# The first two modulation vectors of a two-block transformer: summed without a stop, with products of zeros between their sums over partitions

## The chip, the cores and the metric

The kernel runs on one core of a Trainium2 chip. The metric is device time of one execution in microseconds (us); lower is better. The engines go by the profile's names: PE is the tensor engine (PEld its loads of stationary operands), DVE the vector engine, ACT the scalar engine, POOL the GpSimd engine, and SPq, POOLq and ACTq are the queues from which transfers are issued. Each engine works through its own list of instructions in the order of the program and waits where an operand is not there yet.

## What is computed

Two transformer blocks of two layers each work on 256 tokens of width 1024. Each layer has a mixer and a feed-forward part, and ahead of each of them the normalized activations are scaled and shifted by vectors that come from a condition `c`:

```python
def modulation(c, w, b):
    m = jnp.einsum("bd,de->be", jax.nn.silu(c), w) + b
    shift, scale, gate = jnp.split(m, 3, axis=-1)
...
x = layer_norm(x, ln0_g, ln0_b)
for layer in range(DEPTH):
    shift, scale, gate = modulation(c, ada_w[layer, 0], ada_b[layer, 0])
    h = x * (1.0 + scale) + shift
    y = hybrid_mixer(h, ...)
    x = layer_norm(DN_ALPHA * x + (1.0 + gate) * y, ...)
    ...
```

The first mixer cannot begin before the first `scale` and `shift` are known. Each is a product of a vector of 1024 with a matrix of 1024 x 1024, that is 4 MB of `ada_w` in float32.

## The kernel before

Nine steps follow each other: step 0 is the start (constants, `x`, its layer norm, the first two vectors), steps 1 to 8 are the mixers and feed-forward parts. Nothing of step 1's products can run before step 0's vectors are there.

A vector is made in two parts. `mod_rows` (L282) loads a tile of two 128-row slices of `ada_w` (1 MB, one of four buffers `raw`), and DVE multiplies each slice by its 128 values of silu(`c`) (`csil`) and adds it to the accumulator `macc`: the first slice with a TENSOR_SCALAR (L300), the other seven with a SCALAR_TENSOR_TENSOR (L302), each over 128 x 1024 elements. Then `mod_done` (L304) sums `macc` over the partitions with eight products with a column of ones on PE (L329 to L331, shown under the helper's line L179), and DVE adds the bias to the eight columns (L335, tile `col`). In step 0 `scale` goes first, then `shift`. A `raw` buffer is free again when DVE has read it, so the transfer of a later tile, `w_in` of the mixer among them, waits for DVE.

`setup` (L343) loads the constants and the many small vectors. POOL issues the transfers of most of them, row by row into stacked tiles `sh`; PE transposes each stack (L183) and DVE copies it into a tile of columns (L387): `col3` at once, and `col1`, `col2`, `col4` after the generator's `yield`. `col1` holds the layer norm's gains, which the mixer's scale needs. Behind them stand a mask (`maskb`: a MEMSET on POOL, L410, then two CASTs of DVE into it, L411 and L412) and a few small operations.

In step 1 `ab` (L517) makes A and B from the two vectors and `col1` (L524, L528, L529), `make_h` (L494) makes the mixer's input `h` from the transposed activations (ACT L511 and L513, DVE L509 and L514), and `proj_nat` begins with the products L174 to L176 of `h` with the first tile of `w_in`, which ACT and DVE have split into `hi` (L155) and `lo` (L156).

The program's text does not fix the order on each engine: a scheduler takes instructions by the place of their text, by priorities set around it and by its own costs, and that order is then fixed for the chip. A transfer that POOL issues goes on one of eight semaphores in turn, so the ninth waits until the first has landed.

Of the kernel before, what the change touches and what calls it, by code (L numbers as in the profile page):

```python
# [14 lines left out]
ACT = mybir.ActivationFunctionType  # L15
ALU = mybir.AluOpType
# [4 lines left out]
KD = 8  # L21
# [42 lines left out]
class _Net:  # L64
# [111 lines left out]
        mm(out, lhsT=a[1], rhs=b[0], start=False, stop=stop)  # L176

    def mm(self, out, lhsT, rhs, start=True, stop=True):
        self.nc.tensor.matmul(out, lhsT=lhsT, rhs=rhs, start=start, stop=stop)  # L179

    def tr(self, out, in_):
        p = in_.shape[0]
# [96 lines left out]
        if k0 == 4:  # L279
            self.plus(key, g[:, hs], self.modps)  # L280

    def mod_rows(self, key):  # L282

        nc = self.nc
        V = nc.vector
        w, b, j, c0 = self.mod_src(key)
        row = key[2] == "gate"
        if self.modpos == 0:
            self.modacc = self.tl("macc", [128, D])
            if row:  # L290
                nc.gpsimd.memset(self.modacc, 0.0)
                nc.gpsimd.dma_start(out=self.modacc[0:1, :], in_=b[j * D:(j + 1) * D].unsqueeze(0))
        acc = self.modacc
        wv = w.rearrange("(k p) n -> p k n", p=128)
        v = self.raw(wv[:, self.modpos:self.modpos + 2, j * D:(j + 1) * D])
        for i in range(2):
            k = self.modpos + i
            c = self.csil[:, c0 + k:c0 + k + 1]
            if k == 0 and not row:
                V.tensor_scalar(acc, v[:, i], c, None, ALU.mult)  # L300
            else:
                V.scalar_tensor_tensor(acc, v[:, i], c, acc, ALU.mult, ALU.add)  # L302

    def mod_done(self, key):  # L304

        if key in self.gates_pe:
            return self.modacc
        l, s, name = key
        j, acc = self.mod_src(key)[2], self.modacc
        if name == "gate":  # L310
            g = self.tl("gate", [128, D])
            for h in range(2):
                hs = slice(h * 512, (h + 1) * 512)
                p = self.ps(pool=self.mps)
                self.mm(p, self.ones, acc[:, hs])
                self.plus(key, g[:, hs], p)
            return g
        c = self.tl("col", [128, KD])
        if self.step in (2, 6):

            sums = self.sc([128, KD])
            for k in range(0, KD, 4):
                p = self.ps((128, 4, 128), pool=self.mps)
                for q in range(4):
                    self.tr(p[:, q], acc[:, (k + q) * 128:(k + q + 1) * 128])
                for q in range(4):
                    self.nc.scalar.activation(p[:, q], p[:, q], ACT.Copy, accum_out=sums[:, k + q:k + q + 1])
        else:
            p = self.ps(pool=self.mps)  # L329
            for k in range(KD):  # L330
                self.mm(p[:, k:k + 1], acc[:, k * 128:(k + 1) * 128], self.ones[:, 0:1])  # L331
            sums = p[:, 0:KD]
        q = ((l * 2 + s) * 3 + j) * KD if l < 2 else ((l - 2) * 6 + j) * KD
        bc = (self.col3 if l < 2 else self.col4)[:, q:q + KD]
        self.nc.vector.scalar_tensor_tensor(c, sums, 1.0 if name == "scale" else 0.0, bc, ALU.add, ALU.add)  # L335
        return c

    def mod(self, l, s, name):
        assert (l, s, name) in self.mods, (l, s, name)
        return self.mods[(l, s, name)]  # L340


    def setup(self):  # L343
        nc, a = self.nc, self.a
        S, V = nc.scalar, nc.vector
        cr = self.tl("const", [16, 128], tag="cr")
        S.dma_start(out=cr[0:8], in_=a["c"].rearrange("b (k p) -> (b k) p", p=128))
        S.dma_start(out=cr[8:16], in_=a["c_2"].rearrange("b (k p) -> (b k) p", p=128))
        cst = self.tl("const", [128, C_END], tag="cst")
        nc.sync.dma_start(out=cst, in_=a["consts"])  # L350
        self.ident = cst[:, C_ID:C_LE]
        self.tri_le = cst[:, C_LE:C_LT]
        self.tri_lt = cst[:, C_LT:C_NEG]
        self.rt = cst[:, C_RT:C_COS]
        self.cosn = cst[:, C_COS:C_SIN].rearrange("p (t d) -> p t d", t=2)
        self.sinn = cst[:, C_SIN:C_INV].rearrange("p (t d) -> p t d", t=2)
        self.cst_inv = cst[:, C_INV:C_IOTA]
        self.iota = cst[:, C_IOTA:C_TIE]
        self.tie = cst[:, C_TIE:C_END]
        self.ones = self.tl("const", [128, 128], tag="ones")  # L360
        nc.gpsimd.memset(self.ones, 1.0)
        self.zero = self.tl("const", [128, 128], BF16, tag="zero")
        nc.gpsimd.memset(self.zero, 0.0)
        p = self.ps()
        self.tr(p[:, 0:16], cr)
        self.csil = self.tl("const", [128, 16], tag="csil")
        S.activation(self.csil, p[:, 0:16], ACT.Silu)
        self.off = {}

        def stack(tag, names, eng):  # L370

            r = self.sc([128, 128])
            q = 0
            for name in names:
                ap = a[name]
                n = int(np.prod(ap.shape)) // 128
                lead = " ".join("abc"[:len(ap.shape) - 1])
                eng.dma_start(out=r[q:q + n], in_=ap.rearrange(f"{lead} (k p) -> ({lead} k) p", p=128))
                self.off[name] = q
                q += n  # L380
            return r, q

        def columns(tag, r, q):
            p = self.ps()
            self.tr(p[:, 0:q], r[:q])
            c = self.tl("const", [128, q], tag=tag)
            V.tensor_copy(c, p[:, 0:q])  # L387
            return c

        self.col3 = columns("col3", *stack("col3", ("ada_b",), S))  # L390
        r1 = stack("col1", ("ln0_g", "ln0_b", "post_ln_g", "post_ln_b", "norm_mix_2", "norm_ffn_2"), nc.gpsimd)
        r2, q = stack("col2", ("ssd_conv_w", "ssd_conv_b", "ssd_norm_w", "mla_q_norm", "mla_kv_norm", "gm_b_s"), nc.gpsimd)
        q0 = q
        for name in ("moba_q_norm_2", "moba_k_norm_2", "diff_q_norm_2", "diff_k_norm_2", "moba_out_norm_2"):
            for r in range(2):
                nc.gpsimd.dma_start(out=r2[q:q + 2, r * 64:(r + 1) * 64], in_=a[name])
            self.off[name] = q
            q += 2
        nc.gpsimd.dma_start(out=r2[q:q + 2], in_=a["diff_subln_2"])
        self.off["diff_subln_2"] = q  # L400
        q += 2
        r4 = stack("col4", ("b_mod_2",), nc.gpsimd)
        yield
        self.col1 = columns("col1", *r1)
        self.col2 = columns("col2", r2, q)
        self.col4 = columns("col4", *r4)
        self.identb = self.tl("const", [128, 128], BF16, tag="identb")
        V.tensor_copy(self.identb, self.ident)
        self.maskb = self.tl("const", [128, 384], BF16, tag="maskb")
        nc.gpsimd.memset(self.maskb, 0.0)  # L410
        V.tensor_copy(self.maskb[:, 0:128], cst[:, C_NEG:C_RT])  # L411
        V.tensor_copy(self.maskb[:, 256:384], cst[:, C_NEG:C_RT])  # L412
        o = self.off
        V.tensor_scalar(self.col2[:, 0:60], self.col2[:, 0:60], 0.5, None, ALU.mult)
        q0, q1 = o["moba_q_norm_2"], o["moba_out_norm_2"]
        for b in (0, 64):
            V.memset(self.col2[b:b + 16, q0:q1], 1.0)
        for l in range(2):
            c = o["diff_subln_2"] + l
            V.tensor_scalar(self.col2[:, c:c + 1], self.col2[:, c:c + 1], 1.0 - self.lam_init(l), None, ALU.mult)  # L420
# [1075 lines left out]
    def run(self):  # L1496
        a, nc = self.a, self.nc
# [7 lines left out]

        SC, SH, GA = "scale", "shift", "gate"
        plan = {
            0: [(0, 0, SC), (0, 0, SH)],
            1: [(0, 0, GA), (0, 1, SC), (0, 1, SH)],
            2: [(0, 1, GA), (1, 0, SC), (1, 0, SH), (1, 0, GA), (1, 1, SC), (1, 1, SH)],  # L1510
            3: [(1, 1, GA)],
# [9 lines left out]
        with self.phase(sh=12, s1=1, s2=3, pp=4, pa=4):  # L1521
            setup = self.setup()
            next(setup)
            self.mod_start(plan[0])
            x = self.load_x(a["x"])
            xn = x = self.layer_norm(x)
            self.fill(KD * KD)
            for _ in setup:
                pass
            g, b = self.c1("ln0_g", 0), self.c1("ln0_b", 0)  # L1530
            self.later = [lambda x=x: self.affine(x, a["ln0_g"], a["ln0_b"])]
        for s in range(1, 9):
# [5 lines left out]
            with self.phase(**SIZES[s]):  # L1538
# [18 lines left out]
                    get = lambda t, hh: ysum[t][hh]  # L1557
                else:
                    h = self.make_h(xn, A, B)
                    self.mod_start(plan.get(s, []), LAG.get(s, 0))  # L1560
                    if i == 0:
                        get = self.mixer(l, h, FILL[s]) if one else self.attn2(l - 2, h)
# [48 lines left out]
```

## Time and profile before

| | us |
|---|---|
| median of 3 runs | 2075.84 |
| lowest and highest | 2075.44, 2078.2 |
| the profiled execution | 2076.8 |
| its span in the trace | 2074.9 |
| PE busy in the span | 1931.9 (93%) |
| span to the first product of the first mixer | 44.65 |
| PE busy in the first 46 us | 13.59 |

The profile is of one execution: every instruction with its start and duration in us from the span's start, and of a waiting engine what ended its wait. A row of the timeline reads: start, duration, engine, line, operation, written tile <- read tiles, shape, count, and in brackets the idle time ahead of it with what ended it. Where a row stands for several instructions, the duration is that of all of them.

### The profile page before, as it was taken

The numbers are of one execution on the slowest core, as the hardware profiler recorded it, in microseconds if no ns is written. First come the engines' busy times: TensorE is split into PE (matmuls) and PEld (weight loads), VectorE is DVE, ScalarE is ACT, GpSimd is POOL, SyncE is SP. The second block draws the span as 40 slices with busy tenths as digits, with TensorE's granted clock in tenths as the row PEclk, the third lists the DMA queues.
The fourth block names the chain that finished last, engine by engine and source line by source line (L and its number), as shares of the span: only waits on it lengthen the run. The fifth ranks groups of instructions, "written<-read, shape, count | busy, mean of one in ns | idle before, by whom it ended". The sixth has DMA issues, their size and how long they took to land.

```text
span 2074.9 us, 30043 instructions
## 1 busy us (share of the span) xinstructions
PE 1931.9 (93%) x11481; PEld 1664.2 (80%) x11481; DVE 1656.2 (80%) x2512; ACT 1206.9 (58%) x1817; POOL 49.9 (2%) x100
## 2 busy tenths in 40 slices
PE   3998999898599999999999999969989999998999
PEld 3887999886478787878778887858869998978998
DVE  6888987897598888888888888889778887677554
ACT  3454445462378767767776777755554546555442
POOL 4000000100000000000000000000000000000000
PEclk9999999998599999999999999979999999999999
DMA  9586999565489999899999999957339995326652
GB/s 323 183 285 202 342 339 318 186 222 204 143 311 360 341 334 339 321 357 350 341 326 352 348 362 347 366 181 272 133 126 342 346 324 165 123 82 220 206 203 82
DMA packets 283238, 555.25 MB, mean 268 GB/s; under 512 B 10172, under 2 KB 137520, under 8 KB 283088
## 3 DMA queue, kind: packets, MB, share of 16 engines
q1 hardware_dynamic: 280000, 549.49, 74.8%
q0 software_dynamic: 2656, 3.20, 0.9%
q8 instruction: 91, 1.49, 0.3%
q10 hardware_dynamic: 432, 0.58, 0.1%
q14 instruction: 59, 0.48, 0.1%
HBM read 552.19 MB, written 1.05 MB: 267 GB/s over the span
## 4 chain that ended last, share of the span: by engine, by line
PE 61%; DVE 7%; ACT 3%; issue 2%; DMA 1%; ACTq 0%; DVEq 0%
PE pp L175 11%; PE pp L176 11%; PE pp L174 11%; PE pa L642 6%; PE ya L175 4%; PE ya L174 4%; PE ya L176 4%; PE pp L183 3%; DVE lo L156 2%; PE pp L179 1%; PE pj L174 1%; PE pj L175 1%; PE pj L176 1%; PE sa L179 1%; ACT hi L155 1%
## 5 line engine op out<-in xcount | busy, mean ns | idle before, releaser
L156 DVE TENSOR_TENSOR lo<-raw,hi 128x1024 fp32r<-128x1024 f32 x660 | 786.6, 1220 | 167.9 <-ACT hi L155 162.3
L155 ACT CAST hi<-raw 128x1024 fp32r<-128x1024 f32 x660 | 666.8, 1050 | 374.4 <-PE pp L175 133.2
L174 PE MATMUL pp<-h,hi 128*128 128x256 f32 x960 | 270.3, 282 | 0.0
L175 PE MATMUL pp<-h,hi 128*128 128x256 f32 x960 | 267.3, 278 | 0.0
L176 PE MATMUL pp<-h,lo 128*128 128x256 f32 x960 | 267.2, 278 | 0.0
L156 DVE TENSOR_TENSOR lo<-rawx,hi 128x1024 fp32r<-128x1024 f32 x176 | 208.4, 1220 | 40.0 <-ACT hi L155 38.6
L302 DVE SCALAR_TENSOR_TENSOR macc<-raw,const,macc 128x1024 f32<-128x1024 f32 x168 | 215.4, 1282 | 15.8 <-DMA raw<-in_w_mod_dram 9.1
L155 ACT CAST hi<-rawx 128x1024 fp32r<-128x1024 f32 x176 | 176.8, 1050 | 9.3 <-PE pp L176 7.4
L176 PEld LDWEIGHTS pp<-h,lo 128*128 128x128 f32 x960 | 182.1, 190 | 0.0
L175 PEld LDWEIGHTS pp<-h,hi 128*128 128x128 f32 x960 | 180.2, 188 | 1.7 <-issue 1.2
L174 PEld LDWEIGHTS pp<-h,hi 128*128 128x128 f32 x960 | 180.2, 188 | 1.7 <-ACT hi L155 1.2
L174 PE MATMUL pj<-hi,h 128*128 128x256 f32 x576 | 168.8, 294 | 8.6 <-ACT h L513 3.7
L175 PE MATMUL pp<-lo,h 128*128 128x512 f32 (+1 forms) x480 | 174.9, 365 | 1.3 <-DVE lo L156 1.0
L174 PE MATMUL pp<-hi,h 128*128 128x512 f32 (+1 forms) x480 | 173.0, 361 | 0.0
L175 PE MATMUL pj<-lo,h 128*128 128x256 f32 x576 | 165.2, 288 | 1.1 <-DVE lo L156 1.0
L176 PE MATMUL pj<-hi,h 128*128 128x256 f32 x576 | 164.9, 288 | 0.0
L642 PE MATMUL pa<-hi,s 128*128 128x512 f32 x528 | 148.2, 389 | 0.0
L175 PE MATMUL pp<-lo,xe 128*128 128x512 f32 (+1 forms) x384 | 144.9, 377 | 1.2 <-DVE lo L156 1.0
L174 PE MATMUL pp<-hi,xe 128*128 128x512 f32 (+1 forms) x384 | 143.5, 374 | 0.0
L176 PE MATMUL pp<-hi,x 128*128 128x512 f32 (+1 forms) x384 | 143.5, 374 | 0.0
L176 PE MATMUL pp<-hi,xe 128*128 128x512 f32 (+1 forms) x384 | 143.1, 373 | 0.0
L175 PE MATMUL ya<-lo,s 128*128 128x512 f32 x352 | 140.7, 400 | 0.0
(483 smaller groups left out, 3550.5 us busy)
## 6 DMA issues: line engine op xcount, KB each, us to landing
raw<-in_moe_w_dram SPq DMA_DIRECT2D x176, 1024.0 KB, 6.0
rawx<-in_moe_w_dram SPq DMA_DIRECT2D x88, 1024.0 KB, 6.2
raw<-in_ada_w_dram SPq DMA_DIRECT2D x48, 1024.0 KB, 7.1
raw<-in_w_mod_dram SPq DMA_DIRECT2D x48, 1024.0 KB, 6.5
raw<-in_w_in_dram SPq DMA_DIRECT2D x42, 1024.0 KB, 5.8
raw<-in_ffn_w_dram SPq DMA_DIRECT2D x33, 1024.0 KB, 7.4
raw<-in_w_gate_dram SPq DMA_DIRECT2D x22, 1024.0 KB, 5.3
raw<-in_w_up_dram SPq DMA_DIRECT2D x22, 1024.0 KB, 5.9
```

Source lines behind the costliest of these rows:

```text
L155: self.nc.scalar.copy(h, v[:, z:z + m])
L156: self.nc.vector.tensor_tensor(l, v[:, z:z + m], h.bitcast(F32), ALU.subtract)
L174: mm(out, lhsT=a[0], rhs=b[0], start=start, stop=False)
L175: mm(out, lhsT=a[0], rhs=b[1], start=False, stop=False)
L176: mm(out, lhsT=a[1], rhs=b[0], start=False, stop=stop)
L179: self.nc.tensor.matmul(out, lhsT=lhsT, rhs=rhs, start=start, stop=stop)
L183: self.nc.tensor.transpose(out, in_, self.ident[:p, :p])
L302: V.scalar_tensor_tensor(acc, v[:, i], c, acc, ALU.mult, ALU.add)
L642: mm(accs[t][h], lhsT=y[ia][:, s], rhs=W[ib][:, h * 512:(h + 1) * 512], start=start and ia == 0 and ib == 0, stop=stop and ia == 1)
```

## The change

`mod_first` takes the place of the general route for the first two vectors. The first slice of `shift` is multiplied on ACT (L300 of the new text), so that DVE goes from the last slice of `scale` straight to the second slice of `shift`; both bias additions are put behind the last accumulation. Between the sums over partitions of `scale` and of `shift`, PE does 20 products of a tile of zeros (128 x 128 by 128 x 512, bfloat16). `setup` now has two `yield`s: `col1` is made between the vectors, and the rest (`col2`, `col4`, the mask) after `make_h` in the text, at a changed priority. The stacks of small vectors lie in one tile of the pool `lo` and no longer in three of the pool `sh`.

```diff
-    def mod_rows(self, key):
+    def mod_rows(self, key, act=False):
...
-            if k == 0 and not row:
+            if k == 0 and act:
+                nc.scalar.activation(acc, v[:, i], ACT.Copy, scale=c)
+            elif k == 0 and not row:
                 V.tensor_scalar(acc, v[:, i], c, None, ALU.mult)
             else:
-                V.scalar_tensor_tensor(acc, v[:, i], c, acc, ALU.mult, ALU.add)
+                self.mod_last = V.scalar_tensor_tensor(acc, v[:, i], c, acc, ALU.mult, ALU.add)
...
+    def warm(self, p, n, after):
+
+        with self.tc.issue_after(after):
+            for _ in range(n):
+                self.nc.tensor.matmul(p.rearrange("p (q n) -> p q n", n=128), lhsT=self.zero[:, 0:128], rhs=self.zero[:, None, :].to_broadcast([128, 4, 128]), start=True, stop=True)
+
+    def mod_first(self, scale, shift, setup):
+
+        V = self.nc.vector
+        ps = []
+        for key in (scale, shift):
+            for k in range(0, KD, 2):
+                self.modpos = k
+                self.mod_rows(key, key == shift)
+            p = self.ps()
+            for k in range(KD):
+                self.mm(p[:, k:k + 1], self.modacc[:, k * 128:(k + 1) * 128], self.ones[:, 0:1])
+            ps.append(p)
+            if key == scale:
+                self.warm(self.ps(), 20, self.pe_last.ins)
+                next(setup)
+        for key, p in zip((scale, shift), ps):
+            with self.tc.issue_after(self.mod_last.ins):
+                self.mods[key] = self.mod_col(key, p[:, 0:KD])
...
+        vecs = self.tl("lo", [128, 1024])
         def stack(tag, names, eng):
-            r = self.sc([128, 128])
+            r = vecs[:, len(self.off2) * 128:(len(self.off2) + 1) * 128]
+            self.off2.append(tag)
...
         self.col1 = columns("col1", *r1)
+        yield
         self.col2 = columns("col2", r2, q)
...
-            self.fill(KD * KD)
-            for _ in setup:
-                pass
+            self.mod_first((0, 0, SC), (0, 0, SH), setup)
...
                     h = self.make_h(xn, A, B)
+                    with self.tc.high_priority(offset=-40):
+                        for _ in setup:
+                            pass
```

What this does to the order shows at three places. In all of them `macc` is the accumulator, `raw` a tile of `ada_w`, and `const_113` the tile with the constants.

On DVE, in step 0, from the last slices of `scale` to the last of `shift`. Before:

```order
L302 SCALAR_TENSOR_TENSOR macc_214<-raw_227,const_121,macc_214 128x1024 x2
L335 SCALAR_TENSOR_TENSOR col_231<-pp_232,const_127 128x8
L300 TENSOR_SCALAR macc_242<-raw_243,const_121 128x1024
L302 SCALAR_TENSOR_TENSOR macc_242<-raw_243,const_121,macc_242 128x1024
L302 SCALAR_TENSOR_TENSOR macc_242<-raw_247,const_121,macc_242 128x1024 x2
L302 SCALAR_TENSOR_TENSOR macc_242<-raw_251,const_121,macc_242 128x1024 x2
L302 SCALAR_TENSOR_TENSOR macc_242<-raw_255,const_121,macc_242 128x1024 x2
L335 SCALAR_TENSOR_TENSOR col_259<-pp_260,const_127 128x8
```

On DVE in the changed kernel, the same stretch (`const_410` is the mask, `const_260` the columns `col1`):

```order
L304 SCALAR_TENSOR_TENSOR macc_211<-raw_224,const_121,macc_211 128x1024
L446 CAST const_410<-const_113 128x128
L304 SCALAR_TENSOR_TENSOR macc_211<-raw_224,const_121,macc_211 128x1024
L447 CAST const_410<-const_113 128x128
L304 SCALAR_TENSOR_TENSOR macc_262<-raw_263,const_121,macc_262 128x1024
L304 SCALAR_TENSOR_TENSOR macc_262<-raw_267,const_121,macc_262 128x1024 x2
L421 COPY const_260<-pp_258 128x112
L304 SCALAR_TENSOR_TENSOR macc_262<-raw_271,const_121,macc_262 128x1024 x2
L304 SCALAR_TENSOR_TENSOR macc_262<-raw_275,const_121,macc_262 128x1024 x2
L342 SCALAR_TENSOR_TENSOR col_288<-pp_228,const_127 128x8
L342 SCALAR_TENSOR_TENSOR col_290<-pp_279,const_127 128x8
```

The bias addition of `scale` has left its place between the vectors; a CAST into the mask now stands ahead of the last slice of `scale`, and the copy of `col1` in the middle of `shift`.

On POOL, the MEMSET that clears the mask. Before, it stood ahead of all transfers:

```order
L361 MEMSET const_115 128x128
L363 MEMSET const_117 128x128
L410 MEMSET const_284 128x384
L761 MEMSET cx_583 128x3
L761 MEMSET cx_619 128x3
L267 DMA gate_969<-in_ada_b_dram 1x16x64
L378 DMA sh_129<-in_ln_g_dram 8x128
```

On POOL in the changed kernel, the rows around the same MEMSET; ahead of them stand the 23 other transfers of the stacks:

```order
L412 DMA lo_123<-in_b_mod_dram 96x128
L769 DMA w_425<-in_mla_w_qb_dram 128x4x96
L769 DMA w_425<-in_mla_w_qb_dram 128x4x16 x2
L769 DMA w_426<-in_mla_w_qb_dram 128x4x96
L769 DMA w_426<-in_mla_w_qb_dram 128x4x16 x2
L771 DMA w_433<-in_mla_w_kvb_dram 128x512
L468 DMA s_437<-in_gm_ln_g_dram 128x256
L468 DMA s_439<-in_gm_ln_b_dram 128x256
L468 DMA t_419<-in_ssd_dt_bias_dram 128x8
L468 DMA t_421<-in_ssd_a_log_dram 128x8
L468 DMA t_423<-in_ssd_d_dram 128x8
L445 MEMSET const_410 128x384
```

The MEMSET went from ahead of the first transfer to behind the thirty-sixth.

On PE in the changed kernel, step 0 between the sums over partitions of `scale` (`macc_211`) and of `shift` (`macc_262`); `const_117` is the tile of zeros, and the pair with it stands 20 times:

```order
L179 MATMUL pp_228<-const_115,macc_211 128x1 x8
L353 LDWEIGHTS const_117
L353 MATMUL pp_237<-const_117 128x512
...
L183 MATMUL pp_258<-const_113,lo_123 128x112
L179 MATMUL pp_279<-const_115,macc_262 128x1 x8
L183 MATMUL sd_400<-const_113,lo_123 128x94
L183 MATMUL sd_404<-const_113,lo_123 128x96
```

Before, the two sums followed each other and all three transposes of stacks stood behind them; now the zeros and the transpose for `col1` stand between the sums.

## Rows read from the trace of the kernel before

**Rows 1.** The page's part 1: busy time, share and instructions of each engine.

```profile
PE 1931.9 (93%) x11481; PEld 1664.2 (80%) x11481; DVE 1656.2 (80%) x2512; ACT 1206.9 (58%) x1817; POOL 49.9 (2%) x100
```

**Rows 2.** Stretches: length, busy time per engine, granted clock, DMA share, GB/s.

```profile
0.00:46.00 46.00, 13.59 (x58) 11.86 (x59) 28.15 (x60) 14.27 (x25) 21.39 (x48) 1.00 0.94 330
46.00:100.00 54.00, 53.47 (x370) 44.66 (x370) 45.49 (x105) 28.56 (x67) 1.85 (x7) 1.00 0.58 190
```

**Rows 3.** Timeline of DVE in step 0.

```profile
7.04 0.22 DVE L412 CAST const<-const 128x128 bf16<-128x128 f32 x1
...
19.38 2.61 DVE L302 SCALAR_TENSOR_TENSOR macc<-raw,const,macc 128x1024 f32<-128x1024 f32 x2
...
25.71 0.17 DVE L335 SCALAR_TENSOR_TENSOR col<-pp,const 128x8 f32<-128x8 f32 x1 [3.73 <-PE pp L179]
...
26.57 9.21 DVE L302 SCALAR_TENSOR_TENSOR macc<-raw,const,macc 128x1024 f32<-128x1024 f32 x7
...
39.44 0.17 DVE L335 SCALAR_TENSOR_TENSOR col<-pp,const 128x8 f32<-128x8 f32 x1 [3.66 <-PE pp L179]
39.73 0.60 DVE L387 COPY const<-pp 128x112 f32<-128x112 f32 x3
...
41.97 0.16 DVE L529 TENSOR_TENSOR col<-col,col 128x8 f32<-128x8 f32 x1
```

**Rows 4.** Timeline of PE: sums, transposes, the first products of the mixer.

```profile
22.13 3.54 PE L179 MATMUL pp<-const,macc 128*128 128x1 f32 x16 [0.22 <-DVE macc L302]
...
39.27 0.75 PE L183 MATMUL pp<-const,sh 112*128 112x112 f32 x3
...
44.65 0.57 PE L174 MATMUL pj<-hi,h 128*128 128x256 f32 x1
...
45.75 0.41 PE L174 MATMUL pj<-hi,h 128*128 128x256 f32 x1
...
45.96 0.41 PE L175 MATMUL pj<-lo,h 128*128 128x256 f32 x1
...
48.93 0.28 PE L174 MATMUL pj<-hi,h 128*128 128x256 f32 x1
...
49.05 0.28 PE L175 MATMUL pj<-lo,h 128*128 128x256 f32 x1
```

**Rows 5.** Timeline of POOL in step 0: the mask's MEMSET and the transfers it issues.

```profile
1.14 0.42 POOL L410 MEMSET const<- 128x384 bf16 x1
...
1.57 0.63 POOL L267 DMA_DIRECT2D gate<-in_ada_b_dram  x1
2.18 0.55 POOL L378 DMA_DIRECT2D sh<-in_ln_g_dram  x1
...
7.10 0.53 POOL L378 DMA_DIRECT2D sh<-in_ssd_conv_b_dram  x1 [1.38 <-DMA gate<-in_ada_b_dram]
...
19.81 0.53 POOL L433 DMA_DIRECT2D t<-in_ssd_d_dram  x1
40.31 4.47 POOL L734 DMA_DIRECT2D w<-in_mla_w_qb_dram  x6 [19.97 <-PE pp L183]
```

**Rows 6.** The chain that ended last: 24 products of 512 columns in a later step.

```profile
1567.27 5.45 PE pa L642 x24
```

**Rows 7.** Stretches at the end of step 1, columns as in rows 2.

```profile
174.00:176.00 2.00, 0.74 (x4) 0.27 (x2) 1.71 (x8) 2.00 (x3) 0.00 (x0) 1.00 0.01 4
...
178.00:180.00 2.00, 1.56 (x8) 1.44 (x8) 1.83 (x8) 0.52 (x2) 0.00 (x0) 0.65 0.00 0
...
188.00:190.00 2.00, 2.00 (x15) 2.00 (x15) 2.00 (x3) 1.33 (x4) 0.00 (x0) 0.79 1.05 367
```

**Rows 8.** Line L179: duration in ns, least/median/most, first and last start.

```profile
L179 PEld LDWEIGHTS pp<-const,macc x32: 285/333/333, 22.1 to 39.0; 128*128 128x128 f32 x32
...
L179 PEld LDWEIGHTS pa<-const,macc x32: 187/190/192, 139.7 to 170.9; 128*128 128x128 f32 x32
```

**Rows 9.** Timeline of ACT: step 0's last activation, the next table load.

```profile
19.51 1.24 ACT L456 ACTIVATE x<-x,t,t 128x1024 f32<-128x1024 f32 x1 [6.46 <-DVE t L455]
...
58.01 1.28 ACT L779 ACT_TABLE_LOAD   x1
```

More of the change, by code (lines that the diff above doesn't have):

```diff
@@ L178, in mm @@
     def mm(self, out, lhsT, rhs, start=True, stop=True):
-        self.nc.tensor.matmul(out, lhsT=lhsT, rhs=rhs, start=start, stop=stop)
+        self.pe_last = self.nc.tensor.matmul(out, lhsT=lhsT, rhs=rhs, start=start, stop=stop)
     def tr(self, out, in_):
@@ L317, in mod_done @@
             return g
-        c = self.tl("col", [128, KD])
         if self.step in (2, 6):
@@ L332, in mod_done, with mod_col @@
             sums = p[:, 0:KD]
+        return self.mod_col(key, sums)
+    def mod_col(self, key, sums):
+        l, s, name = key
+        j = self.mod_src(key)[2]
+        c = self.tl("col", [128, KD])
         q = ((l * 2 + s) * 3 + j) * KD if l < 2 else ((l - 2) * 6 + j) * KD
@@ L367, in setup @@
         S.activation(self.csil, p[:, 0:16], ACT.Silu)
-        self.off = {}
+        self.off, self.off2 = {}, []
+        vecs = self.tl("lo", [128, 1024])
         def stack(tag, names, eng):
-            r = self.sc([128, 128])
+            r = vecs[:, len(self.off2) * 128:(len(self.off2) + 1) * 128]
+            self.off2.append(tag)
             q = 0
@@ L383, in columns @@
         def columns(tag, r, q):
-            p = self.ps()
+            p = self.ps(pool="pp" if "pp" in self.pools else "sd")
             self.tr(p[:, 0:q], r[:q])
@@ L1507, in run @@
         plan = {
-            0: [(0, 0, SC), (0, 0, SH)],
             1: [(0, 0, GA), (0, 1, SC), (0, 1, SH)],
@@ L1523, in run @@
             next(setup)
-            self.mod_start(plan[0])
+            self.mod_start([])
             x = self.load_x(a["x"])
             xn = x = self.layer_norm(x)
-            self.fill(KD * KD)
-            for _ in setup:
-                pass
+            self.mod_first((0, 0, SC), (0, 0, SH), setup)
             g, b = self.c1("ln0_g", 0), self.c1("ln0_b", 0)
```

## The prediction

> **What bounds the kernel now.** I read the busy shares first, then the stretches, then the timelines of step 0. PE is busy for 1931.9 us of a span of 2074.9 [rows 1], so nearly all of the 143 idle microseconds are in a few places, and the start is the largest: in the first 46 us PE works for 13.59, and in the 54 us after that for 53.47 [rows 2]. From the first product of the mixer at 44.65 [rows 4] PE hardly stops, while the transfers take 0.58 of their engines' time [rows 2]. So whatever moves the first product moves the end by as much; there is no slack behind it that would swallow a delay of some microseconds, and none that would eat a gain.
>
> What sets 44.65 is one chain on DVE and PE. DVE finishes `scale` at 21.99 and then stands for 3.73 us, because the bias addition waits for the sums on PE; then `shift` takes 0.74 for its first slice and 9.21 for seven others, to 35.78; the sums take another 3.66, and the bias addition of `shift` starts at 39.44 [rows 3]. From there to the first product are 5.2 us more: copies and small operations of the setup, A and B (done at 42.13), and the making of `h` [rows 3, 4].
>
> **The change part by part.** All times are on the profiled execution's own clock. It took 2076.8 us, 1.9 more than its span and 1.0 more than the median of the runs; I add the difference to the median.
>
> *What it takes away.* The wait of 3.73 us and the first slice's 0.74 leave DVE: ACT has nothing to do after 20.75 [rows 9] and can take that slice. If nothing else stood in the way, seven slices at 9.21 / 7 = 1.316 each would run from about 22.0 to 31.2, or 31.7 with the two CASTs and the copy at 0.2 each, and `shift` would be summed up 4.1 us earlier than 35.78. The order of the changed kernel does not allow that, at two places.
>
> *First new wait: the mask.* On DVE a CAST into the mask now stands ahead of the last slice of `scale`. It needs the mask cleared by POOL's MEMSET, and that now stands behind 36 transfers. Before, the MEMSET ran at 1.14, ahead of all transfers, and nobody waited for it [rows 5]. How fast does POOL get through 36 transfers? In the trace it issues one in about 0.53, but of eight at a time: the ninth waits until the first has landed (issued at 1.57, landed by 7.10) [rows 5]. The 27 from 2.18 to 20.34 took 18.16 us, so 0.67 each. From 1.2 on, when the last small MEMSET is through, 24 stacks at 0.67 end at 17.3; the six of `mla_w_qb` cost 4.47 together, to 21.8; six more at 0.67 end at 25.8; with the MEMSET's own 0.42 it is 26.2. Bounds: if the last six need only their issue, 25.1; if the last twelve all take 0.79 (landings of 6.3 us, eight in flight), 27.2. DVE comes to the CAST at 20.7, so it stands for 5.5 us, and behind it stand the last slice of `scale`, all of `shift`, and with them the release of the buffer for the eighth tile of `ada_w`. After 26.2 come the CAST (0.22 [rows 3]) and the slice (1.31): `scale` is accumulated at 27.7, not at 21.99. The tile that was held back is needed only after the second wait below, so its transfer is covered.
>
> The Trainium skill, "DMA: Bandwidth & Descriptors", section "Anatomy of one DMA — SWDGE (gpsimd) path", gives such a transfer a fixed cost of about 2.0 us, where the trace shows over 5 us between issue and landing. By the page's figure no transfer here would wait for a landing, and the sum would be that of the fast queue among the rivals; the measured row differs and decides.
>
> *Second new wait: the zeros.* The sums of `scale` take 3.72 from the last slice to the bias addition (21.99 to 25.71 [rows 3, 4]), so they end at 31.4. Then PE does 20 products of zeros over 512 columns, and only behind them the transpose for `col1`; and DVE's copy of `col1` stands in the middle of `shift`, after three of its seven slices. DVE is there at 27.7 + 0.2 + 3 x 1.316 = 31.8 and waits for the end of the zeros. Their price: 24 products of 512 columns took 5.45, so 0.227 each [rows 6], at the upper of the clock's two levels (2.4 GHz). At the lower one (1.2 GHz) it is twice that. The column for the clock reads 1.00 in the first 46 us, but the first products of the mixer start 0.21 apart at 45.75 and 0.12 apart at 48.93 [rows 4], so PE began there at the lower level and rose some 4 us after the first product. Later the same is seen with the column: the clock falls after PE stops at 174.74, and is back within 188 to 190 [rows 7]. So I let 4.1 us of zeros (9 of them) run at the lower level and 11 at 0.227: 6.6 us in all, bounds 4.5 (all fast) and 9.1 (all slow). The zeros end at 38.0, transpose and copy take 0.4 and 0.27 (three took 0.75 and 0.60 [rows 3, 4]): 38.7. Four slices more: 5.26, to 44.0.
>
> *What the zeros are for.* Loads at the upper level take 190 ns and not 333 [rows 8], so 16 of them would be 2.3 us shorter. But between the end of the zeros and the sums of `shift` PE stands for 5.5 us; after PE's stop at 174.74 the clock had fallen by the stretch from 178 to 180, which reads 0.65 [rows 7]. I count no gain: 3.66 as before, to 47.6.
>
> *The tail.* From the bias addition of `shift` to the first product 5.2 us passed. The new order has A and B right behind it, some 2 us earlier than L529 stood; but the rest of the setup and the whole split of the first weights (1.22) now stand between B and the first piece of `h`, and the second half of that weight tile is split behind `h`, where PE can come to wait for it. I take the sum as zero, bounds -1.0 and +1.0.
>
> *The sum.* The bias addition of `shift` starts at 47.6, not 39.44: 8.2 us later. In step 1 the order changes in many places, and ACT gets two table loads more (1.28 each [rows 9]); ACT is busy for 28.56 of 54 us there [rows 2], so I count them as covered, at most 2.6 if neither is. Forecast: 2076.8 + 8.2 = 2085.0 for the profiled execution, **2084.0** against the median. Its own bounds: queue -1.1, zeros -2.1, tail -1.0 give +4.0, 2079.8; +1.0, +2.5 and +1.0 give +12.7, 2088.5.
>
> **The rivals.**
> *It does what its name says.* DVE runs through, `shift` is complete at 31.7, 4.1 us earlier, and with the clock held the sums take 2.3 less and the first products up to 1.5: 2068 to 2072. For it: the slices' data have landed by then. Against it: the two rows of DVE's order, which wait for POOL and for PE. It holds only if POOL is through 36 transfers by 20.7, hardly later than it was through 28 before.
> *The queue is fast.* No landing is waited for: 30 transfers at 0.52 and six at 0.745 from 1.2 on end at 21.3, the mask is cleared at 21.7, 4.5 us earlier than in my sum. That leaves +3.7, 2079.6; with the clock held into the sums it is +1.4. Against it: in the trace the waits for landings begin at the ninth transfer [rows 5]. The point from which it decides is a mask cleared before about 22.3: then the time is within 0.2% of before, not slower.
> *The start is hidden.* Something later than the first product sets the end, and the time stays at 2075.8. Against it: PE's 53.47 of 54 us [rows 2].
> *Step 1 suffers too.* The uncovered table loads and the changed order add 2.6 to 6 to the sum: 2086.6 to 2090.
>
> **How the numbers follow.** The forecast has 0.63; the fast queue 0.15; the hidden start 0.04; its name's promise 0.08; the suffering step 0.10. About 0.2%, some 4 us, is what a measurement of this kernel can tell from no change: the three runs lie 2.8 us apart. Slower than 2080.0: 0.63 + 0.10 = 0.73; within 0.2%: 0.19; faster than 2071.7: 0.08. The range takes in the forecast's bounds and most of the fast queue: 2077.5 to 2088.5. It leaves out the promise, the hidden start and part of the last rival.
>
> **What would show it.** In the profile of the changed kernel DVE should have a wait of about 5 us ahead of a CAST, ended by POOL's MEMSET at about 26, and one of about 7 us ahead of the copy of `col1`, ended by PE. The zeros should begin near 31 and their spacing fall from 0.45 to 0.23 on the way. The bias addition of `shift` should stand near 47.6 and the first product of the mixer near 53. The forecast is wrong if POOL's MEMSET runs before 22, if the first product stands before 45, or if PE has new idle time in step 1.

## The result: 0.54% slower

Over six runs each the changed kernel takes 2089.5 us and the kernel before 2077.1: a ratio of 1.0054, 95% interval 1.0043 to 1.0065, or 12.4 us more. The profiled execution took 2089.97 us, with a span of 2087.8 against 2074.9, 12.9 more. The forecast was 8.2 more, with 1.7 to 12.7 as its range. The direction and the place were right; the size is at the range's upper end (the median itself lies 1.0 above it, in runs in which the kernel before was 1.3 slower than when the forecast was made).

The changed kernel's busy time (the page's part 1) and its two stretches (columns as in [rows 2]), which answer to [rows 1, 2]:

```profile
PE 1943.0 (93%) x11501; PEld 1669.0 (80%) x11501; DVE 1655.5 (79%) x2511; ACT 1210.8 (58%) x1820; POOL 50.3 (2%) x100
...
0.00:46.00 46.00, 14.61 (x55) 9.37 (x55) 22.39 (x43) 10.70 (x14) 22.13 (x48) 0.98 0.89 306
46.00:100.00 54.00, 51.35 (x316) 42.98 (x316) 41.86 (x107) 26.50 (x61) 1.49 (x6) 0.83 0.50 167
```

PE's 14.61 us in the first stretch contain 6.6 of zeros; without them it does less there than before. In the second stretch its clock is 0.83, where the row of before reads 1.00.

DVE's timeline from the last slices of `scale` to the bias addition of `shift`, against [rows 3]:

```profile
19.68 1.28 DVE L304 SCALAR_TENSOR_TENSOR macc<-raw,const,macc 128x1024 f32<-128x1024 f32 x1
28.06 0.23 DVE L446 CAST const<-const 128x128 bf16<-128x128 f32 x1 [7.10 <-POOL cx L796]
28.20 1.28 DVE L304 SCALAR_TENSOR_TENSOR macc<-raw,const,macc 128x1024 f32<-128x1024 f32 x1
29.40 0.22 DVE L447 CAST const<-const 128x128 bf16<-128x128 f32 x1
29.53 3.92 DVE L304 SCALAR_TENSOR_TENSOR macc<-raw,const,macc 128x1024 f32<-128x1024 f32 x3
39.72 0.27 DVE L421 COPY const<-pp 128x112 f32<-128x112 f32 x1 [6.27 <-PE pp L183]
39.91 5.24 DVE L304 SCALAR_TENSOR_TENSOR macc<-raw,const,macc 128x1024 f32<-128x1024 f32 x4
45.07 0.16 DVE L342 SCALAR_TENSOR_TENSOR col<-pp,const 128x8 f32<-128x8 f32 x1
48.81 0.17 DVE L342 SCALAR_TENSOR_TENSOR col<-pp,const 128x8 f32<-128x8 f32 x1 [3.59 <-PE pp L179]
```

Both forecast waits are there, 7.10 ahead of the CAST and 6.27 ahead of the copy of `col1`; the 3.6 us before the last row are the sums of `shift`, as before. POOL's timeline names the first one's cause: the MEMSET of the mask runs only when the queue has waited for landings of `mla_w_qb`.

```profile
24.44 0.54 POOL L468 DMA_DIRECT2D s<-in_gm_ln_b_dram  x1 [1.36 <-DMA w<-in_mla_w_qb_dram]
...
27.07 0.54 POOL L468 DMA_DIRECT2D t<-in_ssd_d_dram  x1 [0.91 <-DMA w<-in_mla_w_qb_dram]
27.59 0.44 POOL L445 MEMSET const<- 128x384 bf16 x1
```

PE's timeline, against [rows 4]: the sums of `scale`, the zeros, the transpose for `col1`, the sums of `shift`, the first and the twelfth product of the mixer, the gate's bias products (products with one row of stationary operand, of step 1), the thirteenth product that follows them, and the first product of the next projection.

```profile
29.63 3.55 PE L179 MATMUL pp<-const,macc 128*128 128x1 f32 x16 [7.41 <-DVE const L447]
33.03 6.56 PE L353 MATMUL pp<-const 128*128 128x512 bf16 x20
39.42 0.26 PE L183 MATMUL pp<-const,lo 112*128 112x112 f32 x1
45.20 3.57 PE L179 MATMUL pp<-const,macc 128*128 128x1 f32 x16 [5.52 <-DVE macc L304]
...
52.62 0.56 PE L174 MATMUL pj<-hi,h 128*128 128x256 f32 x1
...
55.32 0.41 PE L176 MATMUL pj<-hi,h 128*128 128x256 f32 x1
55.66 3.78 PE L179 MATMUL pa<-gate,const 1*128 1x512 f32 x4
59.37 0.58 PE L174 MATMUL pj<-hi,h 128*128 128x256 f32 x1
...
71.69 0.28 PE L174 MATMUL pj<-h,hi 128*128 128x256 f32 x1
```

The first product is 7.97 us later than 44.65. The other 4.9 of the span's 12.9 arise behind it. Stretches of two microseconds show the clock there (the number before DMA share and GB/s is the granted clock):

```profile
44.00:46.00 2.00, 0.80 (x4) 0.80 (x4) 1.23 (x2) 0.00 (x0) 0.00 (x0) 0.52 1.02 339
...
52.00:54.00 2.00, 2.00 (x9) 1.87 (x10) 1.11 (x3) 2.00 (x6) 0.00 (x0) 0.50 0.00 0
...
62.00:64.00 2.00, 2.00 (x11) 2.00 (x11) 1.28 (x2) 0.00 (x0) 0.00 (x0) 0.50 1.09 317
64.00:66.00 2.00, 2.00 (x17) 2.00 (x16) 0.00 (x0) 1.05 (x1) 0.00 (x0) 0.86 0.96 348
```

After the first product the clock stays at its lower level (0.50, 1.2 GHz) for 11.9 us; before, products at the lower spacing ran for 4.2 us [rows 4]. PE's records show where the time goes in the mixer's first projection, 96 products in both kernels. The twelfth, the thirteenth and the first product of the next projection stood before at:

```profile
47.45 0.41 PE L176 MATMUL pj<-hi,h 128*128 128x256 f32 x1
47.67 0.41 PE L174 MATMUL pj<-hi,h 128*128 128x256 f32 x1
...
58.12 0.28 PE L174 MATMUL pj<-h,hi 128*128 128x256 f32 x1
```

The projection takes 19.07 us and not 13.47, which is 5.6 more. Between the twelfth and the thirteenth product, where the gate's products now stand, 4.05 us pass and not 0.22. From the thirteenth on it is 12.32 and not 10.45, because products run 0.21 apart until 64.4.

I also compared the starts of the same DVE and ACT instructions in both traces: the median lag is 7.9 us between 44 and 51, some 12 between 52 and 72, some 16 between 200 and 1400, and 12.9 at the end. Some 3 us of it come back near 1430 and 1900, as 2 to 3 do in ten of the twelve experiments' traces against this one trace of before, so they probably belong to that execution rather than to the change.

### The profile page after: what moved, and what is told of

The parts are those of the page before. It is cut to its first block, busy times and chain, and to the rows that moved or that the text cites. A ratio compares the mean times of both kernels' runs of the same rounds, so it can differ in the third digit from the quotient of the medians.

```text
span 2087.8 us, 30083 instructions
## 1 busy us (share of the span) xinstructions
PE 1943.0 (93%) x11501; PEld 1669.0 (80%) x11501; DVE 1655.5 (79%) x2511; ACT 1210.8 (58%) x1820; POOL 50.3 (2%) x100
## 4 chain that ended last, share of the span: by engine, by line
PE 61%; DVE 6%; ACT 2%; issue 2%; DMA 0%; ACTq 0%; DVEq 0%
PE pp L175 11%; PE pp L176 11%; PE pp L174 11%; PE pa L677 6%; PE ya L175 4%; PE ya L174 4%; PE ya L176 4%; PE pp L183 3%; DVE lo L156 2%; PE pj L174 2%; PE pj L175 1%; PE pj L176 1%; PE pp L179 1%; PE sa L179 1%; ACT hi L155 1%
```

## Experiments

Each kernel is an edit of the changed kernel unless it says otherwise. Ratios are to the kernel before, run on the same chip beside it. Leaving the zeros out leaves out nothing that an output depends on.

### The two waits, one at a time

The mask first (e1_mask_early):

```diff
         nc.gpsimd.memset(self.zero, 0.0)
+        self.maskb = self.tl("const", [128, 384], BF16, tag="maskb")
+        nc.gpsimd.memset(self.maskb, 0.0)
```

> The changed kernel with the mask cleared at the head of POOL's queue, ahead of all transfers; nothing else moves but the two CASTs of the mask, which go to the head of DVE's order. Theory (two waits on DVE): the wait of 7.10 us that POOL ended is gone, scale is accumulated near 22 and not at 29.5, the zeros end near 32.5, the copy of col1 stands near 33 and not at 39.7, and the first product of the mixer comes 6.5 to 7.1 us earlier, at about 45.6 to 46.1; the span is 6 to 7 us shorter than the changed kernel's 2087.8, about 2081. Rival (the wait only hid the loading of ada_w): DVE stands as long for the data of the last slices, and the first product stays within 1 us of 52.6. Rival (the added time is not in the start): the first product comes 7 us earlier and the span stays above 2086.

Measured: 1.0027 (1.0016 to 1.0038), so about half of the loss is gone. The first product stands at 45.38, 7.2 us earlier: the price of the first wait. The span of the profiled execution, the shortest of seven, is 2076.4. But DVE does not simply run on:

```profile
22.56 1.29 DVE L304 SCALAR_TENSOR_TENSOR macc<-raw,const,macc 128x1024 f32<-128x1024 f32 x1 [0.59 <-ACT macc L300]
26.11 2.60 DVE L304 SCALAR_TENSOR_TENSOR macc<-raw,const,macc 128x1024 f32<-128x1024 f32 x2 [2.26 <-DMA raw<-in_ada_w_dram]
31.94 0.28 DVE L423 COPY const<-pp 128x112 f32<-128x112 f32 x1 [3.23 <-PE pp L183]
32.13 2.60 DVE L304 SCALAR_TENSOR_TENSOR macc<-raw,const,macc 128x1024 f32<-128x1024 f32 x2
35.29 2.60 DVE L304 SCALAR_TENSOR_TENSOR macc<-raw,const,macc 128x1024 f32<-128x1024 f32 x2 [0.56 <-DMA raw<-in_ada_w_dram]
```

The second and the last row wait for transfers of `ada_w` (2.26 and 0.56 us), a wait that the slices of `shift` did not have before [rows 3]. I had not expected that.

Next, no zeros and the mask still late (e2_no_zeros), and both edits, mask first and no zeros (e4_mask_early_no_zeros):

```diff
             if key == scale:
-                self.warm(self.ps(), 20, self.pe_last.ins)
                 next(setup)
```

> The changed kernel without the 20 products of zeros (the mask still late); on DVE the copy of col1 moves up by two slices. Theory: the transposition of col1 follows the sums of scale at about 33.3, DVE is stopped some 2.5 us instead of 6.3, and the first product comes 3.5 to 4 us earlier, near 49; the clock is as late as with zeros (low until some 11 us after the first product), so the span is about 2084. Rival (the zeros use up the upper clock level and so cost the mixer's first products): the clock rises within about 4 us of the first product, as in the kernel before, and the span is 4 us shorter still, about 2080. Rival (the zeros hold the clock for the sums of shift): sums and first products run slower than with zeros, and the span stays near 2087.

> Both of the above: mask cleared first and no zeros; the copy of col1 stands behind more slices of shift and has no one to wait for. Theory: DVE goes through scale and shift without a stop of over 1 us, shift is accumulated near 31.5, its sums end near 35.3, and the first product comes at about 39 to 40, if the first weights of the mixer have landed by then; the span is 13 us below the changed kernel's, 2074 to 2076, because some 4.5 us lost in step 1 remain. Rival (the data bind): the first tile of w_in, which lands at 38.3 in the changed kernel, or the slices of ada_w stop the chain, and the first product is not before 43. Rival (nothing is lost in step 1 once the start is right): the span is 2069 to 2071.

Without zeros: 1.0051 (1.0038 to 1.0064), not to be told from the changed kernel's 1.0054. The first product stands at 51.96, 0.7 earlier, and not near 49. There are two reasons. In this execution POOL cleared the mask at 29.6 and not 28.0; and the scheduler put the copy of `col1` ahead of all seven slices of `shift` that DVE does, where it waits 3.88 us for the sums of `scale`, which PE does first. The transpose behind PE's sums stops DVE with or without zeros. The clock rose 2.5 us after the first product, fell at 58 and rose at 61.4, neither as late as theory nor as clean as the rival had it.

Both edits: 1.0035 (1.0022 to 1.0048), first product 45.07. My expectation of 39 to 40 was wrong. The copy of `col1` does have to wait here too, and behind it the rival "the data bind" shows. DVE's last slices:

```profile
26.93 0.27 DVE L422 COPY const<-pp 128x112 f32<-128x112 f32 x1 [4.02 <-PE pp L183]
27.13 6.56 DVE L304 SCALAR_TENSOR_TENSOR macc<-raw,const,macc 128x1024 f32<-128x1024 f32 x5
34.98 2.61 DVE L304 SCALAR_TENSOR_TENSOR macc<-raw,const,macc 128x1024 f32<-128x1024 f32 x2 [1.30 <-DMA raw<-in_ada_w_dram]
```

DVE stands 4.02 us for the transpose, does five slices in a row, and then the eighth tile has not landed. Which of the two sets the first product this run alone doesn't tell.

### A third cause: traffic that came forward

In the kernel before, POOL's transfers of `mla_w_qb`, `mla_w_kvb` and `gm_ln` start at 40.31 [rows 5], and that row's group waits 19.97 us for PE's transposes of the stacks. My reading, which the next run tests: they go into memory in which the stacks `sh` lay, and PE had to read these first. The change put the stacks into the pool `lo`, so nothing holds those transfers, and POOL issues them at 17.5 to 25, in the midst of `ada_w`. The time from issue to landing of the eighth tile (the issues in the stretch 21.9 to 23; first the kernel before, then e1_mask_early, where it was issued at the same moment, 22.0):

```profile
raw<-in_ada_w_dram SPq DMA_DIRECT2D x1, 1024.0 KB, 6.9
```
```profile
raw<-in_ada_w_dram SPq DMA_DIRECT2D x1, 1024.0 KB, 13.2
```

To test this alone, e5_before_traffic_early is the kernel before with nothing but the stacks moved (and the mask cleared first, as there); PE keeps its order, and so do DVE and ACT in step 0.

```diff
+        vecs = self.tl("lo", [128, 1024])
...
-            r = self.sc([128, 128])
+            r = vecs[:, len(self.off2) * 128:(len(self.off2) + 1) * 128]
+            self.off2.append(tag)
```

> The kernel before, in which only the small vectors are gathered in a buffer of the lo pool, and the mask is cleared first; the orders of PE, DVE and ACT are those of the kernel before, and POOL's transfers of mla_w_qb, mla_w_kvb and gm_ln no longer wait for PE. Theory (that traffic delays ada_w): POOL issues them at 17.5 to 25, the eighth tile of ada_w lands at 34 to 35, DVE waits for it, shift is accumulated at 37.4 and not at 35.8, and the first product comes 1.5 to 2 us later than 44.65; the span is 2075.5 to 2077. Rival (the delayed landings in the changed kernel come from the late release of its buffers): the eighth tile lands by 30, as before, and nothing moves.

Measured: 1.0014 (1.0003 to 1.0024). The transfers came forward, the eighth tile took 12.1 us, and DVE waited for it; POOL, DVE and PE:

```profile
18.70 4.49 POOL L736 DMA_DIRECT2D w<-in_mla_w_qb_dram  x6
```
```profile
34.76 2.60 DVE L302 SCALAR_TENSOR_TENSOR macc<-raw,const,macc 128x1024 f32<-128x1024 f32 x2 [1.03 <-DMA raw<-in_ada_w_dram]
```
```profile
46.24 0.58 PE L174 MATMUL pj<-hi,h 128*128 128x256 f32 x1
```

The first product is 1.6 us later than 44.65. So the traffic alone costs even the old order something. In the new order the first product stood at 45.4 and 45.1 in the two kernels so far with the mask first (e1_mask_early, e4_mask_early_no_zeros).

Then what the change's name promises, a sum without a stop: first with the traffic early (e3_no_dve_wait: mask first, zeros kept, `col1` after all slices), then with the traffic held until `shift` is accumulated (e9_traffic_held):

```diff
-                next(setup)
+        next(setup)
         for key, p in zip((scale, shift), ps):
```
```diff
         wq = [self.tl("w", [128, 4, 128]) for _ in range(2)]
+        if l == 0:
+            for t in wq:
+                V.tensor_copy(t[:, 0, 0:128:16], self.shift_acc[:, 0:8])
```

(`shift_acc` is the accumulated `shift`; the same small copy goes ahead of the transfers of `mla_w_kvb` and the two of `gm_ln`).

> The changed kernel with the mask cleared first, and with col1 transposed and copied only after all slices of shift; the zeros stay. On DVE nothing then stands between the slices. New theory, from the three kernels before this one (the transfers that POOL issues at 17.5 to 25 instead of 40 take the DMA engines from ada_w, so its eighth tile lands near 35 and not at 29): DVE waits for data some 5 us in all, shift is accumulated at 37.6, the first product stands at 44.5 to 45.4 as in the kernel without zeros, and the span is 2073 to 2077, level with the kernel before. Rival (the two waits were all there was): DVE goes through without a stop, shift is accumulated near 31.7, the first product stands near 39.5, and the span is 2069 to 2071.

> The kernel without a wait on DVE (mask first, col1 last, zeros kept), in which POOL's transfers of mla_w_qb, mla_w_kvb and gm_ln are held until shift is accumulated: five copies of 8 columns on DVE, taken from the accumulated shift, stand ahead of them. Theory: the tiles of ada_w land at about 24, 26.5 and 29, as in the kernel before; DVE goes on without a stop over 1 us, shift is accumulated at 31.7 to 32.5, the bias addition of shift stands at 34 to 36, and the first product at 38 to 40; the span is 5 us below 2074.9 or more, 2067 to 2071. Rival (the transfers held back bind in step 1): the first product comes as early, but PE waits later for mla_w_qb, mla_w_kvb or gm_ln, and the span stays above 2073.

e3_no_dve_wait: 1.0013 (1.0002 to 1.0024). DVE waits only for data, 1.90, 2.42 and 2.08 us at three tiles, and the last slices start at 35.18. The new theory holds for DVE: with its two waits removed the changed kernel is still no faster than before. The first product I had too early: two of the gate's products (2.07 us, from 45.61) stand ahead of it, and it comes at 47.60 and not by 45.4.

e9_traffic_held: 0.9975 (0.9960 to 0.9990), the first kernel here that is faster. Its DVE, POOL and PE:

```profile
23.94 7.89 DVE L304 SCALAR_TENSOR_TENSOR macc<-raw,const,macc 128x1024 f32<-128x1024 f32 x6 [0.49 <-DMA raw<-in_ada_w_dram]
```
```profile
32.33 4.46 POOL L775 DMA_DIRECT2D w<-in_mla_w_qb_dram  x6 [12.42 <-DVE s L470]
```
```profile
25.39 7.12 PE L353 MATMUL pp<-const 128*128 128x512 bf16 x20
32.34 1.84 PE L179 MATMUL pp<-const,macc 128*128 128x1 f32 x16
...
38.36 2.07 PE L179 MATMUL pa<-gate,const 1*128 1x512 f32 x2
40.36 0.58 PE L174 MATMUL pj<-hi,h 128*128 128x256 f32 x1
```

DVE does six slices without a stop, the eighth tile lands after 7.2 us, and the sums of `shift` follow the zeros at once and take 1.84 us, not 3.6. The first product, behind two of the gate's products, is 4.3 us earlier than before.

What the zeros are worth there (e10_traffic_held_no_zeros), and what the second wait alone costs there (e11_traffic_held_col1_in_shift: `next(setup)` back in the loop, as in the changed kernel):

> As the kernel with the traffic held, without the products of zeros. Theory (the zeros, ending where the sums of shift begin, keep the upper clock level there): without them the sums of shift take 3.6 us and not 1.9, and the first product comes 1.7 us later, at 40 to 41.5; the span is 2 to 4 us above the one with zeros. Rival (the zeros are worth nothing here either): sums and first product stand within 0.3 us of the kernel with zeros.

> The kernel with the traffic held, but with col1 transposed behind the zeros and copied in the midst of shift, as in the changed kernel (the mask stays first). Theory (this wait alone is worth as much as the traffic, and both end at the same place): the tiles of ada_w land by 29 as in the kernel with the traffic held, DVE stands before the copy of col1 until the zeros are through, near 32.5, four slices follow to 38, the sums of shift take 3.6 us and not 1.8, and the first product stands at 44 to 46 instead of 40.4; the span is 4 to 6 us above that kernel's, 2074 to 2080. Rival (with the data there, DVE goes through the copy without a stop): as the kernel with the traffic held, within 1 us.

Without zeros: 0.9991 (0.9980 to 1.0002) against 0.9975 with them on the same chip. The two intervals overlap, so what the zeros are worth is read from the traces: the sums take 3.57 us, 1.73 more, and the first product stands at 42.76, 2.4 later. With `col1` in the midst of `shift`: 1.0022 (1.0012 to 1.0031), against 0.9977 (0.9968 to 0.9986) for the same kernel without this wait, which was run again beside it (e9_again); 9.0 us between the medians, where I had expected 4 to 6. The first product is at 45.92 and not 40.49. The row of the wait:

```profile
32.92 0.27 DVE L424 COPY const<-pp 128x112 f32<-128x112 f32 x1 [5.89 <-PE pp L183]
```

So there are three things: the mask behind the queue, `col1` behind the zeros, and the traffic in front of `ada_w`. Each of the last two alone keeps the first product at 45 or later (e11_traffic_held_col1_in_shift, e3_no_dve_wait). The mask was not run alone, since it stands behind that traffic; that it would do the same, with `scale` accumulated at 29.4 and seven slices to follow, is argued and not shown. Each hides behind another, and taking away one or two shows little.

### What is lost behind the first product

The changed kernel's gate products held until the first projection is through (e6_gate_held; the order of step 1 is then nearly that of before), and the same on top of the held traffic (e12_traffic_gate_held):

```diff
         if k0 == 0:
             self.modps = self.ps(pool="pa")
-            self.mm(self.modps, self.ones[0:1, :], g[0:1, hs], True, False)
+            with self.tc.issue_after(self.hold):
+                self.mm(self.modps, self.ones[0:1, :], g[0:1, hs], True, False)
```

> The changed kernel with the first bias products of the gate (two products of one row, 3.78 us between products 12 and 13 of the mixer) held behind the first projection; the order of step 1 is then that of the kernel before but for two products. Theory (these products and the order that they bring cost the 4.5 us that the start's 8.0 doesn't explain): the first product stays at 52.6, products 13 and on begin when the second half of the first weights is split, about 58.2 and not 59.4, the clock rises some 4 to 6 us after, and the span is 2 to 4.5 us below 2087.8. Rival (the clock falls because of the waits before the first product, whatever comes between): PE stands idle in place of the four records, the clock rises no earlier than 64, and the span is at most 1.2 us shorter. Rival (zeros): no change at all.

> The kernel with the traffic held, with the first bias products of the gate held behind the first projection too (its four records of 2.07 us in all each two stand ahead of and within the first products at 38.36 and 43.22). Theory (they cost their own time where PE waits for nothing else, and delay the rise of the clock): the first product at 38.3 to 38.6 instead of 40.36, and the clock up some 3 to 6 us earlier than 50; the span 2 to 4 us below that of the kernel with the traffic held. Rival (PE stands for the second half of the first weights in their place, and the clock is as late): the span within 1 us of it, as holding them did nothing in the changed kernel.

e6_gate_held: 1.0072 (1.0059 to 1.0085), no gain. (Its first product stood at 55.00, 2.4 later than in the changed kernel, with the mask cleared at 29.6; so the time alone does not show what holding the gate did.) PE stands in place of the four records:

```profile
57.61 0.28 PE L176 MATMUL pj<-hi,h 128*128 128x256 f32 x1
59.30 0.39 PE L174 MATMUL pj<-hi,h 128*128 128x256 f32 x1 [1.41 <-ACT hi L155]
60.57 0.39 PE L175 MATMUL pj<-lo,h 128*128 128x256 f32 x1 [0.88 <-DVE lo L156]
```

The second half of the first weights is split behind `h`, and PE waits for both its parts. The clock was up at 57.5, 2.5 us after this kernel's first product, fell during these stops (products 0.21 apart again from 60.91), and was up for good at 64.3. The first projection takes 16.97 us, 2.1 less than with the gate's products in it and still 3.5 more than before. So these products are not the whole cause; they fill most of a stop that is there without them. Likewise e12_traffic_gate_held: 0.9981 (0.9972 to 0.9991) against 0.9977, with stops of 0.92 and 0.88 at the same two places, and 16.73 us for the projection. That is what the rival had.

With both halves split ahead of `h` on top of that (e13_split_first):

```diff
-        W = self.wcol(w, c0)
+        with self.tc.high_priority(offset=400) if self.step == 1 and c0 == 1280 else nullcontext():
+            W = self.wcol(w, c0)
```

> As the kernel with traffic and gate held, with both halves of the first weights split ahead of h, as in the kernel before (ACT has nothing to do between 33 and 36). Theory (the second half, split behind h, stops PE for some 3 us after the twelfth product, and that stop also keeps the clock down): the first product 1 us later for the second half on DVE, near 39.5, then no stop of PE over 0.5 us until 60, the clock up by 44 to 45; at 50 to 75 the kernel is 4 to 5 us ahead of the kernel before, and the span is 2068 to 2070. Rival (the clock rises no earlier whatever the order): PE without a stop, but low until 50, and at 50 to 75 less than 2 us ahead of the kernel before.

Measured: 0.9971 (0.9961 to 0.9980), the lowest ratio here, 2070.0 against 2076.3 us. The first product is at 39.64, 5.0 us ahead of before, PE has no stop behind it, and the clock is up early:

```profile
42.00:44.00 2.00, 2.00 (x13) 2.00 (x13) 1.44 (x3) 2.00 (x5) 0.11 (x1) 0.61 1.01 322
44.00:46.00 2.00, 2.00 (x19) 2.00 (x19) 2.00 (x3) 2.00 (x4) 0.00 (x0) 1.00 1.10 358
```

The matched instructions lead by 5.2 us between 50 and 75, and by 4.5 to 5.5 up to 1400: nothing is lost behind the first product, and the first projection takes 13.26 us. e12_traffic_gate_held led by 6.1 at its first product and by 4.0 between 50 and 75. By time the two cannot be told apart (their intervals overlap); by trace the step fits the stop as the cause of some 2 us.

How much the clock adds differs between executions of one kernel. The granted clock of the traffic-held kernel in its first profile and in e9_again, whose first products lie 0.13 us apart:

```profile
44.00:46.00 2.00, 2.00 (x5) 0.78 (x4) 2.00 (x2) 2.00 (x3) 0.00 (x0) 0.50 1.06 323
...
50.00:52.00 2.00, 2.00 (x14) 2.00 (x13) 0.00 (x0) 1.05 (x1) 0.00 (x0) 0.69 1.01 396
```
```profile
44.00:46.00 2.00, 2.00 (x12) 1.28 (x11) 2.00 (x2) 2.00 (x3) 0.00 (x0) 0.99 1.04 319
```

The clock is up at 50 to 52 in the first and at 44 in the second, for which I had expected it to be low until 50 again. The first projection takes 17.55 and 14.23 us, and the spans are 2073.9 and 2070.6: with one order of instructions, both differ by 3.3 us. (The first of these executions took 2075.8 us; that kernel's seven runs lie between 2069.0 and 2076.4.)

## Why the prediction was right, and where it was not

- *The mask.* Right, and mis-sized: cleared at 28.0, forecast 26.2 with 27.2 as the bound. The first thirty transfers went as forecast (to 22.0, forecast 21.8). The term of 0.67 for each of the last six was too small, and so was the bound's 0.79: they took 0.93 each, because landings of `mla_w_qb` took 6.6 to 6.8 us, not 6.3, and POOL stood 1.36 and 0.91 for them. (The lower bound of 25.1 was summed wrong as well: six at 0.53 give 25.4.) In two more executions the mask was cleared at 29.6. DVE stood 7.10, not 5.5.
- *The zeros and `col1`.* Right: 6.56 us, forecast 6.6; DVE stood 6.27, forecast about 6.6. Their spacing fell on the way, as forecast: in the changed kernel five, six and eleven of these products are in work in the stretches 33 to 35, 35 to 37 and 37 to 39.
- *Four slices and sums.* 5.24 and 3.6 us, forecast 5.26 and 3.66; no gain for the sums, since PE stood 5.52 us ahead of them.
- *The tail.* The bias addition stood at 48.81, 1.2 later than forecast; the first product at 52.62, 0.2 earlier than the sum has it (44.65 + 8.2). From one to the other it took 3.8 us and not 5.2: the term of zero was -1.4, outside its bounds of 1.0. Two misses cancel in the 7.97 against 8.2, which is luck.
- *Step 1.* This is the term that failed. I counted it as covered, with two table loads as the only risk (2.6). It cost 4.9 us in the profiled execution, so the time came out where the rival "step 1 suffers too" had it (2086.6 to 2090), but by something else: the second half of the first weights behind `h`, which the tail's paragraph named and priced at nothing, and the clock, which stayed low for 11.9 us in place of 4.2. I had let the clock only gain or stay. In the first projection alone 5.6 us are lost: 3.8 between the twelfth and the thirteenth product and 1.9 at the lower clock behind them, less 0.1 ahead of them. That the second half of the weights lies behind the 3.8 is argued from e6_gate_held, where PE stands for it, and e13_split_first, where the stop is gone; in the changed kernel DVE had split it by 58.15 and the gate's products ran on to 59.4, and the split alone was not tried there. The two table loads are there too, at 139.13 and 143.62, and PE stands 0.55 and 0.57 us for ACT around them. Why the lag goes on to 16 and comes back to 12.9 no run here tells. So the size came to the range's upper end through a term that the forecast had at nothing.
- *The rival "it does what its name says"* was priced at 2068 to 2072 with "the slices' data have landed by then" in its favour. In the changed kernel they could not have: the rows on which that rested [rows 5] show `mla_w_qb` at 40.31, and I counted the six transfers' time on POOL but not what their bytes do to `ada_w` when they move to 17.5. With mask, `col1` and traffic all put right (e9_traffic_held, e9_again), 2069.7 and 2072.5 us beside 2076.0 and 2076.3 before, it comes close to its price.

## What to carry over

When a buffer is moved to another pool, look up who waited for the old one: a wait for memory can be what keeps a transfer out of the way of a more urgent one. Filler products paid here only where they ended as the next real products began and no other engine waited for what stood behind them on PE. Where several causes each set the same moment, test the kernel with all of them removed and put them back one at a time; removing one at a time shows little.

## What was not expected of the hardware

- A transfer of 1 MB issued at 22 to 23 takes 6.9 us to land in the kernel before and 12.1 in e5_before_traffic_early; what differs is 1.0 MB that POOL issues between 18.7 and 26 (two transfers of 192 KB, four of 32, one of 256, two of 128). In the stretch from 17 to 29 us, 362 GB/s were moved in the kernel before, 389 in e9_traffic_held, which holds this traffic, and 343 and 344 in e1_mask_early and e5_before_traffic_early, which do not: with the mixture fewer bytes moved in all.
- The sums of `shift` on PE take 1.84 to 1.95 us right behind the zeros (four traces) and 3.57 to 3.58 after a stop of 5.0 to 11.2 us (ten traces).
- One kernel's clock rose some 4 us after its first product in one execution and some 11 us after it in another, with the same order of instructions.
